# Reordering the first layer of a Fourier / spatial-gating encoder: gate columns, special column and first output block

## The chip, the cores and the metric

The kernel runs on all eight cores of one Trainium2 chip, each core on one sequence of the batch. The metric is the device time of the slowest core, in microseconds. A program on eight cores has executions in a second, slower state (in e1 below, one of 1837.86 us beside three of about 1650); only fast runs are compared here. A ratio below is the mean time of one kernel's fast runs over the mean of the other kernel's fast runs of the same rounds, so it is not quite the ratio of the medians that are quoted beside it. These medians are of the fast runs alone.

## The reference, cut to what matters

```python
def fourier_mixer(h, w_in, w_out):          # layer 0; SEQ 4096, D 1024, E 2048, 8 groups of 256
    proj = h @ w_in
    xin, z = proj[..., :E], proj[..., E:]
    xg = xin.reshape(b, s, 8, 256)
    y = jnp.fft.fft2(xg, axes=(1, 3), norm="ortho").real
    return (y * jax.nn.silu(z)) @ w_out
# layer 1: spatial gating over chunks of 128 positions, w_in (1024, 6144), w_out (2048, 1024)
# before each layer an RMS norm, after each a residual add, at the end an RMS norm
```

The kernel does the Fourier transform with matmuls in two stages: stage 1 over 32 tiles of positions (result U, stored to HBM as Ud), stage 2 after a transposing reload of Ud as V (result H), then for each of eight channel groups a product of H with folded input weights (fold g makes wp from wb; `pq(g)` makes the product). The gate z is 16 columns of channels, each 8 blocks of 8 matmuls (`zall`), with SiLU into one of five buffers `sz`. `gate(g)` multiplies the product into two of these buffers and stores them to HBM as gy. The first output projection (`out0`) reads gy back in blocks of 512 positions as gyt. One real-valued channel per group is a special column, gated apart in `szsp`.

## The kernel before

Only the parts that the change and the argument touch are shown; cuts are marked.

```python
def precast(i):                        # fp32 weights in HBM -> bf16 copies in HBM, software queue
    if i < 2: pool.dma(W0d[:, 8*i:8*i+8, :], w_out0[...], d_pc[i], ...)      # 2 MB written each
    else:     pool.dma(Wind[i-2], w_in1[i-2], d_pc[i], ...)                  # 1 MB written each

for s in range(32):                    # stage 1
    if s + 1 < 32: square(s + 1); norm(s + 1)        # one tile ahead, 3 buffers xn
    # ... 8 transposes, hT, two matmuls with tr, copies to U, store of U ...
    if b8 > 0: zgroup(b8 - 1, s % 2, (s % 8) // 2)   # 8 gate matmuls and a SiLU

def fold(g, dcs):
    # ... matmuls of wb and fmat, copies into wp ...
    if g + 1 < 8: load_wb(2*g + 2); load_wb(2*g + 3) # weights of the next fold, software queue

zall(4)                                # then stage 2: V -> H, eviction in two halves

for g in range(8):
    if g < 7: precast(2*g); precast(2*g + 1)
    # g == 6: special column's gate rows, W0 and x loads
    pq(g); gate(g)
    if g + 1 < 7: fold(g + 1, range(4))
    if g + 2 < 8:
        for zt in (2*g + 4, 2*g + 5):
            if zt > 4: zall(zt)        # gate columns 5.. from group 0 on
    # g == 6: last_column(), gating of szsp on VectorE, its store, load_gy(0, 0, 14)
load_gy(0, 14, 16)                     # then weight ring loads, W1, ...
```

Of the kernel before, what the change touches and what calls it, by code (L numbers as in the profile page):

```python
# [8 lines left out]
BF16 = mybir.dt.bfloat16  # L9
# [178 lines left out]
def build():  # L188
# [30 lines left out]
    with ExitStack() as es:  # L219
# [81 lines left out]
        with ExitStack() as sa:  # L301
# [38 lines left out]
            xn = [tile(f"a0xn{i}", [128, D], BF16) for i in range(3)]  # L340
# [3 lines left out]
            assert top["at"] <= vh + 6 * 8192  # L344
# [5 lines left out]
            wb = [tile("wb0", [128, D], BF16, top["at"] - 2048), tile("wb1", [128, D], BF16)]  # L350
            wp = [tile(f"wp{i}", [128, 8, 256], BF16) for i in range(2)]
# [12 lines left out]
            d_wz = [dsem(f"d_wz{i}") for i in range(4)]  # L364
# [3 lines left out]
            d_sp = dsem("d_sp")  # L368
            zrowb = Buf("zrow")
            Udb = Buf("Ud")  # L370

            def wz_slot(i):
                return i if i < 4 else (i - 4) % 3
# [15 lines left out]
            def square(s):  # L389
                x_, xb = xt[s % NX]  # L390
                j, jb = xn[s % 3]
                ss_, ssb = ss[s % 4]
                act.op(lambda e: e.activation(out=j[:], in_=x_[:], func=AF.Square, scale=1.0 / 32.0,
                                              accum_out=ss_[:]), [xb], [jb, ssb], cost=ca(1024))

            def norm(s):
                x_, xb = xt[s % NX]
                j, jb = xn[s % 3]
# [30 lines left out]
            sp.dma(ident[:], c_id[:, :], d_const, writes=[identb])  # L429
            load_tr(0)  # L430
            load_x(1)
            sp.dma(gT[:], gT_in[:, :], d_cg, writes=[cG])
            load_x(2)
            load_x(3)
            load_tr(1)
            load_x(4)
            sp.dma(cpk[:], c_pk[:, :], d_cA, writes=[cpkb])
            for i in range(4):
                load_wz(i)
            pool.op(lambda e: e.memset(mhalf[:], -0.5), [], [mhalfb])  # L440
            square(0)
            norm(0)
            for s in range(32):
# [3 lines left out]
                if s + 1 < 32:  # L447
                    square(s + 1)
                    norm(s + 1)
                xn_, xnb = xn[s % 3]  # L450
# [17 lines left out]
                sp.dma(Ud[s, 0:128, :], U_[:], d_us[s % 4], reads=[Ub], writes=[Udb])  # L468
                if b8 > 0:
                    zgroup(b8 - 1, s % 2, (s % 8) // 2)  # L470
# [7 lines left out]
            for zt in (3, 0, 1, 2):  # L478
# [5 lines left out]
                else:  # L484
                    load_wz(4 + zt)


            def fold(g, dcs):
                w_, wpb = wp[g % 2]
                for d2 in dcs:  # L490
# [8 lines left out]
                    copy_on(ev_engine(), w_[:, 2 * d2:2 * d2 + 2, :], bank[:].rearrange("p (a b) -> p a b", b=256),  # L499
                            [bb], [wpb])  # L500
                if dcs[-1] == 3:
                    dve.op(lambda e: e.tensor_copy(out=wsp[:, :, g:g + 1], in_=w_[:, :, 128:129]), [wpb], [wspb],
                           waw=False)
                    dve.op(lambda e: e.memset(w_[:, :, 128:129], 0.0), [], [wpb])  # L504
# [4 lines left out]
            def zall(zt):  # L509
# [3 lines left out]
                if zt + 3 < 16:  # L513
                    load_wz(zt + 3)
# [8 lines left out]
            zall(4)  # L523
            for qd in range(7, -1, -1):
                for dc in range(8):
# [8 lines left out]
                    q = ev_engine()  # L534
                    for cs in range(2):
                        scaled(q, H[:, qd, dc, cs, 0:256].rearrange("d (t j k) -> d t j k", j=4, k=2),
                               bank[:].rearrange("d (j c t k) -> d c t j k", c=2, j=4, k=2)[:, cs], sc,
                               [bb, g0sb], [Hb[qd]], 256)
                    if qd == 0:
                        bank, bb = next_f()  # L540
                        pe.op(lambda e: e.matmul(bank[:, 0:64], V[:, 0, dc * 128:(dc + 1) * 128], b64,
                                                 start=True, stop=True), [Vb[0], cpkb], [bb], waw=False)
                        for cs in range(2):
                            scaled(ev_engine(), H[:, :, dc, cs, 256:260],
                                   bank[:, 32 * cs:32 * cs + 32].rearrange("d (q t) -> d q t", t=4), sc, [bb, g0sb],
                                   Hb, 32)
                if qd < 4:
# [3 lines left out]
            def pq(g):  # L551
                w_, wpb = wp[g % 2]
                for qd in range(8):
# [11 lines left out]
                    for o, ob, op in ((Dt, Dtb, ALU.subtract), (St, Stb, ALU.add)):  # L565
                        dve.op(lambda e: e.tensor_tensor(out=o[:, qd, :], in0=pc_[:], in1=bq[:, 0:HQ], op=op),  # L566
                               [pcb, bqb], [ob], waw=False, cost=cd(HQ))

            def gate_tile(o, ob, a_, ab, m_, mb):
# [4 lines left out]
                def mul(out, in0, rb, n):  # L574
                    dve.op(lambda e: e.tensor_tensor(out=out, in0=in0, in1=out, op=ALU.mult), [rb, ob], [ob],
                           waw=False, cost=cd(n))
# [6 lines left out]
            def gate(g):  # L583
                for h, ((a_, ab), (m_, mb)) in enumerate((((Dt, Dtb), (St, Stb)), ((St, Stb), (Dt, Dtb)))):
# [3 lines left out]
                    r0 = (2 * g + h) * 128  # L588
                    sp.dma(gyT[r0:r0 + 128, :], o[:].rearrange("c a b -> c (a b)"), d_gy[i], reads=[ob],
                           writes=[gyTb[2 * g + h]])  # L590

            def last_column():

                for qd in range(8):
# [5 lines left out]
                    copy_on(act, p128[:, qd, :], bank[0:8, 0:HQ], [bb], [p128b], n=HQ)  # L600
# [11 lines left out]
            gytb = [Buf("gyt0", (gyo, gyo + 14336)), Buf("gyt1", (gyo + 14336, gyo + 16384))]  # L612
# [31 lines left out]
            d_g = [dsem(f"d_g{i}") for i in range(2)]  # L644
# [11 lines left out]
            def load_gy(i, k0, k1):  # L656
                bs_ = [gytb[0]] if k1 <= 14 else ([gytb[1]] if k0 >= 14 else gytb)
                sp.dma(gyt[:, k0:k1, :], gyT[k0 * 128:k1 * 128, i * 512:(i + 1) * 512].rearrange(
                    "(kc p) s -> p kc s", p=128), d_g[1 if k0 >= 14 else 0], reads=gyTb[k0:k1], writes=bs_, waw=True)
# [39 lines left out]
            def out0(n, ks, banks):  # L699
                c0 = (n % 4) * 128  # L700
                out_mm(lambda kc: gyt[:, kc, c0:c0 + 128], W0, lambda kc: [gytb[kc // 14]],
                       lambda kc: [W0b[kc // 8]], ks, banks)
# [86 lines left out]

            for g in range(8):  # L790
                if g < 7:
                    precast(2 * g)
                    precast(2 * g + 1)
                if g == 6:
                    sp.dma(szsp[:], zrow.rearrange("g (a b) -> g a b", b=128), d_sp, reads=[zrowb],
                           writes=[szspb], waw=True)
                    for i in range(2):
# [148 lines left out]
```

## Time and profile before

The median of the kernel before was 1708.16 us (1707.06 to 1709.89, three runs). The profiled execution spans 1699.8 us on core 5, the slowest.

The first view shows the busy time of each engine in six stretches of core 5: stage 1 up to the first V load, stage 2 up to the first group product, the groups up to the last gate matmul, the tail up to the first transposition of layer 1, the value tiles of layer 1's first block, and the rest. After the window and its length come busy us and instruction count of each engine, the granted TensorE clock, the DMA share and GB/s.

```profile
core 5: us, PE busy (x) PEld busy (x) DVE busy (x) ACT busy (x) POOL busy (x), PEclk, DMA share, GB/s
0.00:125.30 125.30, 85.18 (x525) 43.01 (x526) 79.17 (x97) 67.63 (x122) 27.90 (x73) 1.00 0.72 221
125.30:195.50 70.20, 51.26 (x397) 28.89 (x396) 27.96 (x75) 35.79 (x90) 4.04 (x8) 0.88 0.66 144
195.50:465.70 270.20, 252.06 (x1570) 154.81 (x1571) 71.10 (x156) 81.86 (x159) 18.06 (x35) 0.96 0.68 131
465.70:564.20 98.50, 69.32 (x465) 45.07 (x464) 33.99 (x62) 15.22 (x35) 4.53 (x9) 0.84 0.80 221
...
595.90:1699.80 1103.90, 1092.52 (x5601) 517.12 (x5599) 536.84 (x782) 305.76 (x505) 89.53 (x178) 1.00 0.36 127
```

The reader sees a kernel bound by TensorE (PE) everywhere but in the first 564 us, where the lengths exceed the PE busy times by 40, 19, 18 and 29 us. Only that is to be won. The waits of PE on the same core say what ended that idle time (total us, number of waits, longest):

```profile
PE pf L681 <- DMA gyt<-gy: 28.3, 2, 15.3
PE pf L415 <- ACT sz_72 L419: 18.1, 1, 18.1
PE pb L454 <- DVE a0xn_57 L405: 17.4, 7, 10.3
PE pb L454 <- DVE a0xn_58 L405: 13.8, 7, 5.7
PE pf L415 <- DMA wz_77<-wz: 12.0, 1, 12.0
...
```

L454 is the transposition of stage 1, which waits for the normalised tile. L415 is a gate matmul: once it waits for its weights (wz), once, for 18.1 us, for a SiLU that itself waits for its buffer. The timeline places that wait after the sixth block of gate column 5, when the six PSUM banks are full (start, length, instruction, count, and in brackets the idle time before it):

```profile
213.14 10.52 PE L415 MATMUL pf<-hT,wz_78 128*128 128x512 bf16 x48
241.79 6.08 PE L415 MATMUL pf<-hT,wz_78 128*128 128x512 bf16 x16 [18.13 <-ACT sz_72 L419]
```

The SiLU waits for the store of the buffer's earlier contents to gy, which was issued at 215.7 us and took 25.3 us to land, beside the two casts of W0. (The casts are the fp32 to bf16 copies of `precast`.) The DMA view has that store; its last number is the time from issue to landing, in us:

```profile
gy<-sz_72 SPq DMA_DIRECT2D x1, 1024.0 KB, 25.3
```

L681 is `out0`, which waits twice for gyt, because the last gate tiles go through HBM and come back.

### The profile page before, as it was taken

How to read it: one execution, taken by the hardware profiler on the slowest of the kernel's cores; microseconds unless marked ns; L12 is line 12 of the kernel's file. 1: busy time of each engine (PE TensorE's matmuls, PEld its weight loads, DVE VectorE, ACT ScalarE, POOL GpSimd, SP SyncE). 2: the span in 40 equal slices, each digit the busy share in tenths (PEclk: the TensorE clock that was granted, in tenths of full speed). 3: DMA queues.
4: the chain of work that ended last, by engine and by line, in shares of the span. 5: the costliest groups of instructions: out<-in, count | busy, mean ns of one | idle time of the engine just before them, and what ended most of it. 6: DMA issues, size and time to landing. Idle time of an engine off the chain costs nothing.

```text
span 1699.8 us, 25579 instructions; the slowest of 8 cores (1683.4 to 1699.8 us)
## 1 busy us (share of the span) xinstructions
PE 1580.3 (93%) x8714; PEld 803.4 (47%) x8714; DVE 768.5 (45%) x1198; ACT 516.9 (30%) x928; POOL 149.1 (9%) x310
## 2 busy tenths in 40 slices
PE   4886859999984999999999999999999999999997
PEld 2443636666672444444444444444444444444443
DVE  5660712222260572464356346345535724643562
ACT  4652613333320332233133123213312322331331
POOL 2220000000000100110110010001001001100100
PEclk9998979999997999999999999999999999999999
DMA  9759485558569553334244325334332533432311
GB/s 259 225 168 228 52 149 125 125 111 168 113 215 199 192 199 136 112 149 161 87 147 149 126 75 190 122 99 171 138 124 87 187 125 99 174 136 87 119 56 50
DMA packets 59854, 239.36 MB, mean 141 GB/s; under 512 B 5688, under 2 KB 22200, under 8 KB 43320
## 3 DMA queue, kind: packets, MB, share of 16 engines
q1 hardware_dynamic: 53968, 208.10, 36.0%
q0 software_dynamic: 5760, 29.63, 11.2%
q8 instruction: 73, 1.20, 0.3%
q14 instruction: 53, 0.43, 0.1%
HBM read 225.26 MB, written 58.85 MB: 167 GB/s over the span
## 4 chain that ended last, share of the span: by engine, by line
PE 83%; DMA 6%; DVE 5%; issue 3%; ACT 1%; POOL 1%; SPq 0%; DVEq 0%; ACTq 0%; POOLq 0%
PE pf L681 25%; PE pf L757 25%; PE pf L415 11%; PE pf L731 10%; PE pf L559 6%; DMA gy<-sz_72 4%; PE pf L767 2%; DMA wz_77<-wz 1%; DMA a0x_54<-xt 1%; DVE H L520 1%; PE pb L716 1%; PE pf L495 1%; PE pb L454 1%; ACT v_2500 L734 0%; ACT v_2499 L734 0%
## 5 line engine op out<-in xcount | busy, mean ns | idle before, releaser
L681 PE MATMUL pf<-W_2474,gyt 128*128 128x512 bf16 x1024 | 228.7, 384 | 28.3 <-DMA gyt<-gy 28.3
L681 PE MATMUL pf<-W_2485,u 128*128 128x512 bf16 x1024 | 222.3, 379 | 0.0
L681 PEld LDWEIGHTS pf<-W_2474,gyt 128*128 128x128 bf16 x1024 | 100.5, 99 | 149.0 <-issue 34.4
L681 PEld LDWEIGHTS pf<-W_2485,u 128*128 128x128 bf16 x1024 | 100.1, 98 | 120.9
L760 ACT ACTIVATE u<-pf 128x512 bf16<-128x512 f32 x128 | 73.8, 599 | 145.1 <-PE pf L757 129.9
L757 PE MATMUL pf<-h1T,ring_2480 128*128 128x512 bf16 x416 | 95.3, 379 | 0.6 <-DVE TT L838 0.6
L757 PE MATMUL pf<-h1T,ring_2481 128*128 128x512 bf16 x416 | 94.8, 379 | 0.0
L757 PE MATMUL pf<-h1T,ring_2483 128*128 128x512 bf16 x416 | 94.8, 379 | 0.0
L757 PE MATMUL pf<-h1T,ring_2484 128*128 128x512 bf16 x416 | 94.8, 379 | 0.0
L415 PE MATMUL pf<-hT,wz_78 128*128 128x512 bf16 x320 | 73.5, 388 | 18.1 <-ACT sz_72 L419 18.1
L757 PE MATMUL pf<-h1T,ring_2482 128*128 128x512 bf16 x384 | 88.3, 379 | 0.0
L415 PE MATMUL pf<-hT,wz_77 128*128 128x512 bf16 x320 | 75.5, 396 | 12.4 <-DMA wz_77<-wz 12.0
L566 DVE TENSOR_TENSOR Dt<-pc_87,pf 128x260 bf16<-128x260 f32 x32 | 13.6, 425 | 153.4 <-PE pf L559 153.4
L415 PE MATMUL pf<-hT,wz_79 128*128 128x512 bf16 x320 | 70.9, 379 | 0.0
L734 ACT ACTIVATE v_2500<-pf 128x512 f32<-128x512 f32 x64 | 38.2, 597 | 74.7 <-DVE sm_2507 L736 33.8
L559 PE MATMUL pf<-H,wp_83 128*128 128x260 bf16 x512 | 59.1, 278 | 1.6 <-DVE wp_83 L504 1.6
L672 POOL TENSOR_SCALAR sm_2506<-sm_2506 128x1 f32<-128x1 f32 x24 | 5.3, 221 | 629.3 <-ACT xn_0_2486 L695 576.4
L757 PEld LDWEIGHTS pf<-h1T,ring_2484 128*128 128x128 bf16 x416 | 39.7, 98 | 43.4
L757 PEld LDWEIGHTS pf<-h1T,ring_2480 128*128 128x128 bf16 x416 | 39.5, 98 | 43.6 <-issue 1.1
L757 PEld LDWEIGHTS pf<-h1T,ring_2483 128*128 128x128 bf16 x416 | 39.6, 98 | 43.2
L757 PEld LDWEIGHTS pf<-h1T,ring_2481 128*128 128x128 bf16 x416 | 39.6, 98 | 43.2
L719 DVE TENSOR_TENSOR h1T<-pb,gTs 128x1024 bf16<-128x1024 bf16 x32 | 38.7, 1208 | 45.6 <-PE pb L716 45.6
(241 smaller groups left out, 2321.7 us busy)
## 6 DMA issues: line engine op xcount, KB each, us to landing
ring_2480<-wind SPq DMA_DIRECT2D x20, 1024.0 KB, 4.9
ring_2481<-wind SPq DMA_DIRECT2D x19, 1024.0 KB, 5.2
ring_2482<-wind SPq DMA_DIRECT2D x19, 1024.0 KB, 5.3
ring_2483<-wind SPq DMA_DIRECT2D x19, 1024.0 KB, 5.2
ring_2484<-wind SPq DMA_DIRECT2D x19, 1024.0 KB, 5.5
gyt<-gy SPq DMA_DIRECT2D x7, 2048.0 KB, 8.5
wind<-w_in1p POOLq DMA_DIRECT2D x12, 1024.0 KB, 14.6
V<-ud SPq DMA_DIRECT2D x32, 256.0 KB, 20.5
```

What stands on the lines that cost most here:

```text
L415: pe.op(lambda e: e.matmul(bank[:], w[:, dc, :], mv[:, :, hf * 64:hf * 64 + 64], start=(dc == 0), stop=(dc == 7)), [wb_, hTb[b8], hTall], ...
L454: pe.op(lambda e: e.transpose(out=bank[:, dc * 128:(dc + 1) * 128], in_=xn_[:, dc * 128:(dc + 1) * 128], identity=ident[:]), [xnb, identb] ...
L495: pe.op(lambda e: e.matmul(bank[:, h * 256:(h + 1) * 256], wb[kc][0][:, dc * 128:(dc + 1) * 128], fmat[:, kc, :], start=(kc == 0), stop=(k ...
L520: return q.op(lambda e: e.tensor_scalar(out=out_ap, in0=in_ap, scalar1=sc, scalar2=None, op0=ALU.mult), reads, writes, waw=False, cost=cd(n))
L559: pe.op(lambda e: e.matmul(bank[:, 0:HQ], w_[:, dc, cs * 128:(cs + 1) * 128], H[:, qd, dc, cs, :], start=(dc == 0), stop=(dc == 7)), [wpb, ...
L681: pe.op(lambda e: e.matmul(bank[:], lhs(kc), rhs[:, kc, nh * 512:(nh + 1) * 512], start=(kc == 0), stop=(kc == 15)), lb(kc) + rb(kc), [bb] ...
L719: dve.op(lambda e: e.tensor_tensor(out=h1T[:, :, t * 128:(t + 1) * 128], in0=bank[:].rearrange("p (a b) -> p a b", b=128), in1=g1T.rearran ...
L731: pe.op(lambda e: e.matmul(bank[:], h1T[:, dc, t * 128:(t + 1) * 128], r_[:, dc, :], start=(dc == 0), stop=(dc == 7)), [h1Tb[t], rb], [bb] ...
L734: act.op(lambda e: e.activation(out=v_[:, j * 512:(j + 1) * 512], in_=bank[:], func=AF.Gelu_apprx_tanh), [bb], [vb_], waw=False)
L757: pe.op(lambda e: e.matmul(bank[:], r_[:, dc, c0:c0 + 128], h1T[:, dc, :], start=(dc == 0), stop=(dc == 7)), h1Tb + [rb], [bb], waw=False, ...
L760: act.op(lambda e: e.activation(out=out_ap, in_=bank[:], func=func), [bb], wb_)
L767: pe.op(lambda e: e.matmul(bank[:, t * 128:(t + 1) * 128], vhat[t][0][:, ct * 128:(ct + 1) * 128], wsT[:, ct // 2, :], start=True, stop=True),
```

## The change

Its intent: normalise two tiles ahead and defer the early loads of stage 1; compute gate column 4 inside stage 2 and evict stage 2 in whole banks; move the gate columns two to a group behind the second product, so that all are done by group 5; do the special column there too, gated on GpSimd; and feed the last four chunks of the first output block from the gate buffers in SBUF. Not shown below: from fold 1 on, the copies of a fold into wp are all on ScalarE, and the small copy into wsp and the clearing of a column of wp that follow it move from VectorE to GpSimd. The core of the diff:

```diff
-            load_tr(0); load_x(1); ... load_tr(1); load_x(4); cpk; four load_wz      (at the start)
+            load_x(1); load_tr(0); load_x(2); ... load_x(4)
+                if s == 2: load_tr(1); four load_wz
+                if s == 24: cpk; load_wz(4)                                           (fifth slot)
-                if s + 1 < 32: square(s + 1); norm(s + 1)
+                if s + 2 < 32: square(s + 2)          ... and norm(s + 2) after the copies to U
...
-            zall(4)
             for qd in range(7, -1, -1):               (stage 2)
-                    two evictions of 256 columns, permuted
+                    one eviction of 512 columns; the permutation moves to the Dt/St writes of pq
+                zgroup((7 - qd) // 2, (7 - qd) % 2, 4)
...
+            zafter = [[], [5, 6], [7, 8], [9, 10], [11, 12], [13, 14, 15], [], []]
+            npre = [0, 2, 4, 6, 9, 12, 14, 14, 14]
             for g in range(8):
-                if g < 7: precast(2 * g); precast(2 * g + 1)
                 pq(g)
                 gate(g)
+                for i in range(npre[g], npre[g + 1]): precast(i)
                 if g + 1 < 7: fold(g + 1, range(4))
-                two gate columns, from g = 0 on
+                for zt in zafter[g]: (fold 7 before column 15) zall(zt)
+                if g == 5: szsp load, last_column(), gating of szsp on pool, W0, load_gy(0, 0, 12), x
...
-            out0: lhs gyt[:, kc, ...]
+            out0: lhs sz[kc % 5] if first block and kc >= 12 else gyt[:, kc, ...]
-            pool.dma(W1 ...), sp.dma(bsB ...)          right after the groups
+            the same two loads after the first output block
```

More of the change, by code (lines that the diff above doesn't have):

```diff
@@ L339, in build @@
             trb = [Buf(f"tr{i}", (top["at"] - 8192 + 2048 * i, top["at"] - 6144 + 2048 * i)) for i in range(4)]
-            xn = [tile(f"a0xn{i}", [128, D], BF16) for i in range(3)]
+            xn = [tile(f"a0xn{i}", [128, D], BF16) for i in range(4)]
             U = [tile(f"U{i}", [128, D], BF16) for i in range(4)]
@@ L343, in build @@
             rs = [tile(f"a0rs{i}", [128, 1], F32) for i in range(4)]
-            assert top["at"] <= vh + 6 * 8192
+            assert top["at"] <= vh + 7 * 8192
             top["at"] = vh + 74752
@@ L350, in build @@
             wb = [tile("wb0", [128, D], BF16, top["at"] - 2048), tile("wb1", [128, D], BF16)]
+            wz.append(tile("wz4", [128, 8, 128], BF16, top["at"] + 4096))
             wp = [tile(f"wp{i}", [128, 8, 256], BF16) for i in range(2)]
@@ L363, in build @@
             d_v = [dsem(f"d_v{i}") for i in range(8)]
-            d_wz = [dsem(f"d_wz{i}") for i in range(4)]
+            d_wz = [dsem(f"d_wz{i}") for i in range(5)]
             d_wb = [dsem(f"d_wb{i}") for i in range(2)]
@@ L368, in build @@
             d_sp = dsem("d_sp")
+            d_row = dsem("d_row")
             zrowb = Buf("zrow")
@@ L372, in wz_slot @@
             def wz_slot(i):
-                return i if i < 4 else (i - 4) % 3
+                return i if i < 5 else (i - 5) % 3
             def load_wz(i):
@@ L390, in square @@
                 x_, xb = xt[s % NX]
-                j, jb = xn[s % 3]
+                j, jb = xn[s % 4]
                 ss_, ssb = ss[s % 4]
@@ L397, in norm @@
                 x_, xb = xt[s % NX]
-                j, jb = xn[s % 3]
+                j, jb = xn[s % 4]
                 ss_, ssb = ss[s % 4]
@@ L429, in build @@
             sp.dma(ident[:], c_id[:, :], d_const, writes=[identb])
+            load_x(1)
             load_tr(0)
-            load_x(1)
+            load_x(2)
             sp.dma(gT[:], gT_in[:, :], d_cg, writes=[cG])
-            load_x(2)
             load_x(3)
-            load_tr(1)
             load_x(4)
-            sp.dma(cpk[:], c_pk[:, :], d_cA, writes=[cpkb])
-            for i in range(4):
-                load_wz(i)
             pool.op(lambda e: e.memset(mhalf[:], -0.5), [], [mhalfb])
@@ L442, in build @@
             norm(0)
+            square(1)
+            norm(1)
             for s in range(32):
@@ L446, in build @@
                     load_x(s + 5)
-                if s + 1 < 32:
-                    square(s + 1)
-                    norm(s + 1)
-                xn_, xnb = xn[s % 3]
+                if s == 2:
+                    load_tr(1)
+                    for i in range(4):
+                        load_wz(i)
+                if s == 24:
+                    sp.dma(cpk[:], c_pk[:, :], d_cA, writes=[cpkb])
+                    load_wz(4)
+                if s + 2 < 32:
+                    square(s + 2)
+                xn_, xnb = xn[s % 4]
                 U_, Ub = U[s % 4]
@@ L468, in build @@
                 sp.dma(Ud[s, 0:128, :], U_[:], d_us[s % 4], reads=[Ub], writes=[Udb])
+                if s + 2 < 32:
+                    norm(s + 2)
                 if b8 > 0:
@@ L484, in build @@
                 else:
-                    load_wz(4 + zt)
+                    load_wz(5 + zt)
             def fold(g, dcs):
@@ L498, in fold @@
                                   [wb[kc][1], cpkb], [bb], waw=False, inc=(h == 1 and kc == 1))
-                    copy_on(ev_engine(), w_[:, 2 * d2:2 * d2 + 2, :], bank[:].rearrange("p (a b) -> p a b", b=256),
+                    copy_on(ev_engine() if g == 0 else act, w_[:, 2 * d2:2 * d2 + 2, :], bank[:].rearrange("p (a b) -> p a b", b=256),
                             [bb], [wpb])
                 if dcs[-1] == 3:
-                    dve.op(lambda e: e.tensor_copy(out=wsp[:, :, g:g + 1], in_=w_[:, :, 128:129]), [wpb], [wspb],
-                           waw=False)
-                    dve.op(lambda e: e.memset(w_[:, :, 128:129], 0.0), [], [wpb])
+                    pool.op(lambda e: e.tensor_copy(out=wsp[:, :, g:g + 1], in_=w_[:, :, 128:129]), [wpb], [wspb],
+                            waw=False)
+                    pool.op(lambda e: e.memset(w_[:, :, 128:129], 0.0), [], [wpb])
                     if g + 1 < 8:
@@ L512, in zall @@
                         zgroup(b8, hf, zt)
-                if zt + 3 < 16:
+                if 5 <= zt < 13:
                     load_wz(zt + 3)
@@ L533, in build @@
                               [Vb[qd], cpkb], [bb], waw=False, inc=(jj == 3))
-                    q = ev_engine()
-                    for cs in range(2):
-                        scaled(q, H[:, qd, dc, cs, 0:256].rearrange("d (t j k) -> d t j k", j=4, k=2),
-                               bank[:].rearrange("d (j c t k) -> d c t j k", c=2, j=4, k=2)[:, cs], sc,
-                               [bb, g0sb], [Hb[qd]], 256)
+                    scaled(ev_engine(), H[:, qd, dc, :, 0:256].rearrange("d c (j k) -> d c j k", j=4),
+                           bank[:].rearrange("d (j c k) -> d c j k", c=2, j=4), sc, [bb, g0sb], [Hb[qd]], 512)
                     if qd == 0:
@@ L542, in build @@
                                                  start=True, stop=True), [Vb[0], cpkb], [bb], waw=False)
+                        q = ev_engine()
                         for cs in range(2):
-                            scaled(ev_engine(), H[:, :, dc, cs, 256:260],
+                            scaled(q, H[:, :, dc, cs, 256:260],
                                    bank[:, 32 * cs:32 * cs + 32].rearrange("d (q t) -> d q t", t=4), sc, [bb, g0sb],
                                    Hb, 32)
+                zgroup((7 - qd) // 2, (7 - qd) % 2, 4)
                 if qd < 4:
@@ L565, in pq, with perm, gate_tile @@
                     for o, ob, op in ((Dt, Dtb, ALU.subtract), (St, Stb, ALU.add)):
-                        dve.op(lambda e: e.tensor_tensor(out=o[:, qd, :], in0=pc_[:], in1=bq[:, 0:HQ], op=op),
-                               [pcb, bqb], [ob], waw=False, cost=cd(HQ))
-            def gate_tile(o, ob, a_, ab, m_, mb):
+                        def perm(t_):
+                            return t_[:, 0:256].rearrange("c (j t k) -> c t j k", j=4, k=2)
+                        dve.op(lambda e: e.tensor_tensor(
+                            out=o[:, qd, 0:256].rearrange("c (t j k) -> c t j k", j=4, k=2), in0=perm(pc_), in1=perm(bq),
+                            op=op), [pcb, bqb], [ob], waw=False, cost=cd(HQ))
+                        dve.op(lambda e: e.tensor_tensor(out=o[:, qd, 256:260], in0=pc_[:, 256:260],
+                                                         in1=bq[:, 256:260], op=op), [pcb, bqb], [ob], waw=False,
+                               cost=0.1)
+            def gate_tile(o, ob, a_, ab, m_, mb, q=dve):
                 def main(t_):
@@ L574, in mul @@
                 def mul(out, in0, rb, n):
-                    dve.op(lambda e: e.tensor_tensor(out=out, in0=in0, in1=out, op=ALU.mult), [rb, ob], [ob],
-                           waw=False, cost=cd(n))
+                    q.op(lambda e: e.tensor_tensor(out=out, in0=in0, in1=out, op=ALU.mult), [rb, ob], [ob],
+                         waw=False, cost=cd(n))
                 mul(o[:, :, 0:64].rearrange("c t (q k) -> c t q k", k=8), main(a_), ab, 2048)
@@ L588, in gate @@
                     r0 = (2 * g + h) * 128
+                    if h == 1 and g >= 6:
+                        sp.dma(o[0:1], szsp[g:g + 1], d_row, reads=[szspb], writes=[ob], waw=True)
                     sp.dma(gyT[r0:r0 + 128, :], o[:].rearrange("c a b -> c (a b)"), d_gy[i], reads=[ob],
@@ L599, in last_column @@
                               [wspb, Hb[qd]], [bb], waw=False, inc=(dc == 7))
-                    copy_on(act, p128[:, qd, :], bank[0:8, 0:HQ], [bb], [p128b], n=HQ)
+                    copy_on(act, p128[:, qd, 0:256].rearrange("c (t j k) -> c t j k", j=4, k=2),
+                            bank[0:8, 0:256].rearrange("c (j t k) -> c t j k", j=4, k=2), [bb], [p128b], n=HQ)
+                    copy_on(act, p128[:, qd, 256:260], bank[0:8, 256:260], [bb], [p128b], n=4)
             def span_tile(name, shape, dtype, off):
@@ L611, in build @@
             gyt, _, _ = at("gyt", [128, 16, 512], BF16, gyo)
-            gytb = [Buf("gyt0", (gyo, gyo + 14336)), Buf("gyt1", (gyo + 14336, gyo + 16384))]
+            gytb = Buf("gyt", (gyo, gyo + 16384))
             NX1 = 5
@@ L643, in build @@
             d_w0 = [dsem(f"d_w0_{i}") for i in range(2)]
-            d_g = [dsem(f"d_g{i}") for i in range(2)]
+            d_g = dsem("d_g")
             d_x1 = [dsem(f"d_x1_{i}") for i in range(NX1)]
@@ L656, in load_gy @@
             def load_gy(i, k0, k1):
-                bs_ = [gytb[0]] if k1 <= 14 else ([gytb[1]] if k0 >= 14 else gytb)
                 sp.dma(gyt[:, k0:k1, :], gyT[k0 * 128:k1 * 128, i * 512:(i + 1) * 512].rearrange(
-                    "(kc p) s -> p kc s", p=128), d_g[1 if k0 >= 14 else 0], reads=gyTb[k0:k1], writes=bs_, waw=True)
+                    "(kc p) s -> p kc s", p=128), d_g, reads=gyTb[k0:k1], writes=[gytb], waw=True)
             NW = 12 * 8
@@ L700, in out0, with here @@
                 c0 = (n % 4) * 128
-                out_mm(lambda kc: gyt[:, kc, c0:c0 + 128], W0, lambda kc: [gytb[kc // 14]],
-                       lambda kc: [W0b[kc // 8]], ks, banks)
+                def here(kc):
+                    return n < 4 and kc >= 12
+                out_mm(lambda kc: sz[kc % 5][0][:].rearrange("c a b -> c (a b)")[:, c0:c0 + 128] if here(kc)
+                       else gyt[:, kc, c0:c0 + 128], W0,
+                       lambda kc: [sz[kc % 5][1]] if here(kc) else [gytb], lambda kc: [W0b[kc // 8]], ks, banks)
             def norm1(n):
@@ L787, in finish_tile @@
                 sp.dma(out[n * 128:(n + 1) * 128, :], x_[:], d_out[n % NX1], reads=[xb], writes=[outb])
+            zafter = [[], [5, 6], [7, 8], [9, 10], [11, 12], [13, 14, 15], [], []]
+            npre = [0, 2, 4, 6, 9, 12, 14, 14, 14]
+            gsp = gyT.rearrange("(g r) s -> g r s", r=256)[:, 128, :]
+            ssp = szsp[:].rearrange("c a b -> c (a b)")
             for g in range(8):
-                if g < 7:
-                    precast(2 * g)
-                    precast(2 * g + 1)
-                if g == 6:
+                pq(g)
+                gate(g)
+                for i in range(npre[g], npre[g + 1]):
+                    precast(i)
+                if g + 1 < 7:
+                    fold(g + 1, range(4))
+                for zt in zafter[g]:
+                    if zt == 15:
+                        fold(7, range(4))
+                    zall(zt)
+                if g == 5:
                     sp.dma(szsp[:], zrow.rearrange("g (a b) -> g a b", b=128), d_sp, reads=[zrowb],
                            writes=[szspb], waw=True)
+                    last_column()
+                    gate_tile(szsp, szspb, p128, p128b, p128, p128b, pool)
                     for i in range(2):
@@ L799, in build @@
                                writes=[W0b[i], hTall])
+                    sp.dma(gsp[0:6], ssp[0:6], d_sp, reads=[szspb], writes=gyTb[1:12:2], waw=True)
+                    load_gy(0, 0, 12)
                     for n in range(4):
                         load_x1(n)
-                pq(g)
-                gate(g)
-                if g + 1 < 7:
-                    fold(g + 1, range(4))
-                if g + 2 < 8:
-                    for zt in (2 * g + 4, 2 * g + 5):
-                        if zt > 4:
-                            zall(zt)
-                if g == 5:
-                    fold(7, range(4))
-                if g == 6:
-                    last_column()
-                    gate_tile(szsp, szspb, p128, p128b, p128, p128b)
-                    gsp = gyT.rearrange("(g r) s -> g r s", r=256)[:, 128, :]
-                    ssp = szsp[:].rearrange("c a b -> c (a b)")
-                    sp.dma(gsp[0:7], ssp[0:7], d_sp, reads=[szspb], writes=gyTb[1:14:2], waw=True)
-                    load_gy(0, 0, 14)
-            sp.dma(gsp[7:8], ssp[7:8], d_sp, reads=[szspb], writes=[gyTb[15]], waw=True)
-            load_gy(0, 14, 16)
             for n in range(NR):
@@ L826, in build @@
             pool.op(lambda e: e.memset(ones[:], 1.0), [], [onesb])
-            pool.dma(W1[:], w_out1[:, :, :], d_w1, writes=[W1b], waw=True)
-            sp.dma(bsB[:], b_s.partition_broadcast(128), d_cB[1], writes=[bsBb], waw=True)
             def tables():
@@ L862, in build @@
                     trans1(2)
+                    sp.dma(bsB[:], b_s.partition_broadcast(128), d_cB[1], writes=[bsBb], waw=True)
+                    pool.dma(W1[:], w_out1[:, :, :], d_w1, writes=[W1b], waw=True)
                 else:
```

## The prediction

> **What bounds the kernel now.** TensorE. The page gives PE 1580 of 1699.8 us; by the windows view PE is busy 1121 of 1133 us from 567 us on (second layer), hardly touched. The other 107 idle us lie in the first 567 us. Waits view and timeline:
> - Transform stage 1, 0 to 123 us: PE 83 us. It waits for normalised tiles (17.4 + 13.8 + 8.3 us), first because x shares the DMA with early weights (landed at 5.6, 14.6, 18.9, 20.8, 25.2 us), then in pairs of 6.73 us, of which PE fills about 5.3: the next square queues on ScalarE behind SiLU.
> - 136.7 to 148.7: 12.0 us on a gate weight load; then 13.8 us of gate matmuls before stage 2, while its V loads run from 125 to 172 us.
> - Stage 2, 165 to 195.5: evictions bound it (DVE 28.0, ACT 27.4, PE 23.2 of 30.1 us).
> - 223.7 to 241.8: 18.1 us. SiLU waits for its buffer's store to gy, which takes 25.3 us beside the W0 cast copies.
> - Tail, 504 to 567: two waits of 13.0 and 15.3 us for gyt, through gate, store and reload.
>
> **What changes, costed.**
> 1. Early loads deferred, normalisation two tiles ahead: first eight tiles about 9 us sooner; later iterations from 3.36 to about 2.85 us (PE needs 2.65, DVE 2.5, ACT 2.45; DMA 768 KB each, estimated 270 GB/s against 306 GB/s seen at 20 to 40 us). Stage 1 ends near 103 instead of 122.7. Gain 19.
> 2. The fifth gate weight has its own slot (12 us wait gone), and that gate column's eight groups of 1.73 us are spread over stage 2, whose 16 half evictions per block (0.37 to 0.40 us) become 8 full ones (about 0.6). Stage 2 then needs 4.7 us of PE per block, about the 5.5 us pace at which V lands. First group product starts near 159, not 195.5. Cumulative gain 36.
> 3. Gate columns move behind the second product, so the 18.1 us wait goes. But the W0 casts (27 and 44.5 us to landing) start with the first product, now without 27 us of gate work to hide them, and the third fold's weights queue behind them on the software queue (30.5 us to landing now). I expect a new wait of about 13 us before fold 2, and 2 us before the second product. Net gain near zero to 5.
> 4. Special column moves before product 6. Its gating moves to GpSimd: the Trainium skill, "GPSIMD Engine Reference", section 3.1, gives 4497 ns for a 2048-element fp32 add; estimate from it about 10 us for 4096 elements, against 5.3 us on DVE here. No run shows this. It should hide under products 6 and 7 (28.4 us), with gyt about 3 us early. Output blocks 0 to 3 read the last four chunks from SBUF, so both gyt waits vanish: gain about 33.
> 5. W1's load moves after the first output block and meets ring loads: loses 0 to 4 us. Permuted Dt/St writes add DVE work off the path.
>
> **Sum.** About 76 us: span near 1624, time **1632 us**, 80% range 1612 to 1656. Faster by over 2%: 0.96; within: 0.03; slower: 0.01.
>
> **What would show it.** V loads begin near 105 us; no gate-weight wait; first product near 159; PE wait before fold 2 on a wb load; no gyt wait over 5 us; second layer's first block near 490.
>
> **What would make it wrong.** Stage 1 being DMA bound (loses 10); a slow GpSimd gate blocking the DMA queue ahead of gyt (5 to 10); W0 casts ending sooner (gains 10); W1 starving the weight ring.

## The result, and the profile after

The changed kernel took 1660.59 us (median of four, 1659.45 to 1663.09) against 1708.49 us for the kernel before (now the median of four runs): ratio 0.9722, 95% interval 0.9705 to 0.9739. It is faster, but 28.6 us slower than predicted and 4.6 us outside the stated range.

The same six stretches on core 7, the slowest of its profiled execution, with the boundaries at the same events:

```profile
core 7: us, PE busy (x) PEld busy (x) DVE busy (x) ACT busy (x) POOL busy (x), PEclk, DMA share, GB/s
0.00:108.40 108.40, 82.02 (x524) 43.78 (x525) 79.28 (x97) 66.41 (x122) 29.88 (x74) 0.94 0.89 258
108.40:166.00 57.60, 48.95 (x399) 29.67 (x397) 22.89 (x38) 33.03 (x62) 3.09 (x7) 0.94 0.79 170
166.00:450.70 284.70, 251.95 (x1585) 155.29 (x1586) 76.48 (x240) 85.50 (x163) 23.35 (x50) 0.95 0.70 125
450.70:518.00 67.30, 64.98 (x449) 43.74 (x448) 30.79 (x88) 13.66 (x39) 12.02 (x12) 0.97 0.74 247
...
549.70:1659.40 1109.70, 1094.61 (x5601) 517.78 (x5599) 537.24 (x782) 306.12 (x506) 89.60 (x178) 0.99 0.36 128
```

| stretch | before, us | after, us | change | predicted change |
|---|---|---|---|---|
| stage 1 | 125.3 | 108.4 | -16.9 | about -20 |
| stage 2 | 70.2 | 57.6 | -12.6 | about -16 |
| groups | 270.2 | 284.7 | +14.5 | 0 to -5 |
| tail | 98.5 | 67.3 | -31.2 | about -33 |
| after it | 1135.6 | 1141.4 | +5.8 | 0 to +4 |

The changes sum to 40.4 us, the difference of the two profiled spans; the timed medians differ by 47.9, since the profiled execution of the kernel before was among its quicker ones. (The last row is the fifth and sixth stretch together. Fold 7, 1.75 us, moved from the tail into the groups, so the groups lost 12.7 us of their own and the tail won 29.5.) The row that is off is the groups. The waits of PE on core 7:

```profile
PE pf L503 <- DMA wb_82<-wbT: 25.8, 1, 25.8
PE pb L460 <- DVE a0xn_57 L407: 17.3, 3, 9.4
PE pf L779 <- DMA ring_2414<-wind: 5.1, 1, 5.1
PE pb L460 <- DVE a0xn_60 L407: 4.9, 2, 4.4
PE pf L503 <- DMA wb_83<-wbT: 3.3, 1, 3.3
...
```

The gyt, SiLU and gate-weight waits are gone. A new one leads: fold 2 (L503) waits 25.8 and 3.3 us for its two weight tiles. The timeline of PE shows it between the second product and column 5 (the 2.20 us before the second product, for the clearing on GpSimd, are the small wait that the prediction named):

```profile
184.27 14.35 PE L565 MATMUL pf<-H,wp_86 128*128 128x260 bf16 x128 [2.20 <-POOL wp_86 L512]
224.46 0.37 PE L503 MATMUL pf<-cpk,wb_82 128*128 128x256 bf16 x1 [25.84 <-DMA wb_82<-wbT]
228.12 0.37 PE L503 MATMUL pf<-cpk,wb_83 128*128 128x256 bf16 x1 [3.29 <-DMA wb_83<-wbT]
...
231.27 14.21 PE L417 MATMUL pf<-hT,wz_78 128*128 128x512 bf16 x64
```

The timeline of GpSimd, which issues the software queue, shows what stands in front of those two loads:

```profile
167.38 1.07 POOL L181 DMA_DIRECT2D w0d<-w_out0p  x2
...
184.46 0.55 POOL L181 DMA_DIRECT2D wb_82<-wbT  x1 [0.45 <-issue]
185.00 0.54 POOL L181 DMA_DIRECT2D wb_83<-wbT  x1
185.53 1.00 POOL L181 DMA_DIRECT2D wind<-w_in1p  x2
```

The DMA view of 184 to 206 us gives the times from issue to landing (the last number, us) of the two weight tiles and of three of the gate stores that run at the same time on the hardware queue:

```profile
...
gy<-sz_73 SPq DMA_DIRECT2D x1, 1024.0 KB, 31.3
gy<-sz_74 SPq DMA_DIRECT2D x1, 1024.0 KB, 35.4
...
gy<-sz_76 SPq DMA_DIRECT2D x1, 1024.0 KB, 39.8
wb_82<-wbT POOLq DMA_DIRECT2D x1, 256.0 KB, 39.7
wb_83<-wbT POOLq DMA_DIRECT2D x1, 256.0 KB, 43.0
```

A 256 KB load that lands in 5.2 us at best in this same kernel took 39.7 us. The cores are not alike in this: 0, 2, 4 and 6 wait 16.6 to 20.1 us before fold 2, and 1, 3, 5 and 7 wait 27.6 to 29.3. In every fast run of this kernel one core of each pair 0/1, 2/3, 4/5, 6/7 ends 7 to 26 us after its neighbour, and not always the same one. The Trainium skill ("Trainium Kernel Development and Optimization", NeuronCore Architecture) gives main storage per pair of cores; the pattern agrees with two cores competing there, but no run here isolates it.

### The profile page after: what moved, and what is told of

It reads as the page before. It is cut to its first block, busy times and chain, and to the rows that moved or that the text cites. A ratio compares the mean times of both kernels' runs of the same rounds, so it can differ in the third digit from the quotient of the medians.

```text
span 1659.4 us, 25674 instructions; the slowest of 8 cores (1633.4 to 1659.4 us)
## 1 busy us (share of the span) xinstructions
PE 1572.5 (95%) x8714; PEld 804.7 (48%) x8714; DVE 766.1 (46%) x1271; ACT 515.4 (31%) x907; POOL 163.7 (10%) x330
## 4 chain that ended last, share of the span: by engine, by line
PE 86%; DMA 7%; DVE 3%; issue 1%; ACT 1%; SPq 1%; POOL 0%; DVEq 0%; ACTq 0%; POOLq 0%
PE pf L697 27%; PE pf L779 25%; PE pf L417 11%; PE pf L753 11%; PE pf L565 6%; DMA wb_83<-wbT 3%; PE pf L789 2%; DMA V<-ud 1%; DMA ring_2414<-wind 1%; DMA a0x_52<-xt 1%; PE pf L503 1%; PE pb L738 1%; SPq L181 1%; DMA a0x_50<-xt 1%; DMA gTs<-gT 1%
## 5 line engine op out<-in xcount | busy, mean ns | idle before, releaser
L697 PE MATMUL pf<-W_2408,gyt 128*128 128x512 bf16 x992 | 218.8, 379 | 0.0
L697 PEld LDWEIGHTS pf<-W_2408,gyt 128*128 128x128 bf16 x992 | 96.6, 98 | 113.4
L575 DVE TENSOR_TENSOR Dt<-pc_89,pf 128x256 bf16<-128x256 f32 x32 | 13.5, 421 | 198.1 <-PE pf L565 198.1
L417 PE MATMUL pf<-hT,wz_78 128*128 128x512 bf16 x320 | 72.2, 384 | 0.0
L417 PE MATMUL pf<-hT,wz_79 128*128 128x512 bf16 x320 | 70.9, 379 | 0.0
L756 ACT ACTIVATE v_2434<-pf 128x512 f32<-128x512 f32 x64 | 38.2, 598 | 75.3 <-DVE sm_2441 L758 34.1
L779 PEld LDWEIGHTS pf<-h1T,ring_2418 128*128 128x128 bf16 x416 | 39.7, 98 | 43.4
L779 PEld LDWEIGHTS pf<-h1T,ring_2415 128*128 128x128 bf16 x416 | 39.7, 98 | 43.2
L793 DVE SCALAR_TENSOR_TENSOR ytmp_2427<-pf,gTs,TT 128x512 f32<-128x512 f32 x64 | 48.1, 751 | 24.8 <-PE pf L789 24.8
L782 ACT ACTIVATE sg_2436<-pf 128x512 bf16<-128x512 f32 x64 | 38.3, 598 | 68.0 <-PE pf L779 54.7
```

Source lines behind the costliest of these rows:

```text
L417: pe.op(lambda e: e.matmul(bank[:], w[:, dc, :], mv[:, :, hf * 64:hf * 64 + 64], start=(dc == 0), stop=(dc == 7)), [wb_, hTb[b8], hTall], ...
L697: pe.op(lambda e: e.matmul(bank[:], lhs(kc), rhs[:, kc, nh * 512:(nh + 1) * 512], start=(kc == 0), stop=(kc == 15)), lb(kc) + rb(kc), [bb] ...
L756: act.op(lambda e: e.activation(out=v_[:, j * 512:(j + 1) * 512], in_=bank[:], func=AF.Gelu_apprx_tanh), [bb], [vb_], waw=False)
L779: pe.op(lambda e: e.matmul(bank[:], r_[:, dc, c0:c0 + 128], h1T[:, dc, :], start=(dc == 0), stop=(dc == 7)), h1Tb + [rb], [bb], waw=False, ...
L782: act.op(lambda e: e.activation(out=out_ap, in_=bank[:], func=func), [bb], wb_)
L793: dve.op(lambda e: e.scalar_tensor_tensor(out=y_[:].rearrange("c (t p) -> c t p", p=128), in0=bank[:].rearrange("c (t p) -> c t p", p=128) ...
```

## The experiments

The theory, called Q: the wait before fold 2 is queueing. The weights stand behind the W0 casts on one software queue, and the casts are slower than I had costed because the gate stores now run beside all of them. The rival, B: the stretch is bound by the bytes of casts and stores together, so that another order only moves the wait. Beside these, one part of the change was undone at a time to see what each was worth. Each diff is against the changed kernel unless it says otherwise. Of fourteen kernels, all were correct but e3, which is wrong on purpose. In the trace lines of the experiments, buffer numbers are left out by the profile.

### e1: casts one group later

```diff
-npre = [0, 2, 4, 6, 9, 12, 14, 14, 14]
+npre = [0, 0, 2, 4, 6, 9, 12, 14, 14]
```

> The changed kernel with the W0 casts issued one group later, so that the weights of fold 2 stand in front of them on the software queue; same bytes, same engines' work. Theory Q (the 29 us wait before fold 2 on the slowest core is queueing behind the casts): that wait falls below 3 us; the gate stores now meet the casts, so SiLU may wait up to 10 us for its buffer; time 1633 to 1645. Rival B (the stretch is bound by the bytes that stores and casts move): the wait only moves to SiLU or to another load, 20 us or more, time 1655 to 1663.

Measured: 1652.00 us (three fast runs, one slow), ratio 0.9695 (0.9666 to 0.9724). The waits of core 7, the slowest:

```profile
PE pf L697 <- DMA gyt<-gy: 10.1, 1, 10.1
PE pf L697 <- DMA sz<-szsp: 5.7, 1, 5.7
...
PE pf L503 <- DMA wb<-wbT: 2.7, 2, 1.8
```

The weight wait fell from 29 to 2.7 us, as Q says, but the time fell by little, as B says. The reason can be read off: the shift had pushed the last two casts into group 6, behind the gating of the special column on GpSimd (issued at 443.0 us), where they delayed the store of the special rows; gyt could be requested only at 464.7 us. The test had a flaw, so its time did not decide. Its trace does show the queueing. On core 7 the weights of fold 2 were issued at 181.7 us, 1 us before the two W0 casts, and landed early (median of the two tiles):

```profile
wb<-wbT POOLq DMA_DIRECT2D x2, 256.0 KB, 8.4
```

That is 8.4 us in front of the same casts, against 39.7 and 43.0 us behind them in the changed kernel.

### e2: one cast in front instead of two

```diff
+npre = [0, 1, 3, 5, 7, 10, 12, 14, 14]
```

> Only one of the two W0 casts stays in front of fold 2's weights. Q: the wait falls by about the time of one cast (17 to 24 us) to 5 to 12 us; time 1640 to 1650. B: the wait stays above 20 us, because the same bytes are on the way in this stretch.

Measured: 1646.96 us, ratio 0.9666 (0.9643 to 0.9689). The weight waits were at most 4.6 us, below what Q expected, and the tail had the same gyt wait as e1 (9.0 us on core 1, the slowest), from the same flaw (its last two casts are in group 6 as well).

### e3: no gate stores in groups 0 and 1 (wrong result on purpose)

```diff
+                    if g >= 2:
                         sp.dma(gyT[r0:r0 + 128, :], o[:]..., d_gy[i], ...)
-                gyt[:, k0:k1] <- gyT rows of chunks k0..k1
+                gyt[:, 0:4] and gyt[:, 4:k1] <- gyT rows of chunks 4..7 and 4..k1
```

> The four gate stores of groups 0 and 1 left out (wrong result on purpose; the loads of the output blocks read other rows instead, same bytes), queue order as in the changed kernel. Q: the wait before fold 2 shrinks only by what the stores slow the casts, from 29 to 15 to 22 us; time 1646 to 1654. B: it falls below 8 us; time below 1642.

Measured: 1645.11 us, ratio 0.9658 (0.9637 to 0.968), just under the time that Q had given. On core 6, the slowest:

```profile
PE pf L503 <- DMA wb<-wbT: 15.5, 2, 13.9
```

With the queue order unchanged and only the four stores gone, the weight wait is 15.5 to 17.1 us on the slower core of each pair and 9.7 to 12.3 on the other. So about 13 us of the 29 came from the stores, and about 15 from the casts alone. On the slower cores this is the range Q had given for the wait, and far from B's 8 us.

What the stores slow can be read from the times to landing of the W0 tensors. The last number is the longest, that of the later W0 cast: first core 7 of the changed kernel, then core 6 of e3.

```profile
DMA to landing us min/median/max: 8.8/18.2/51.8
DMA to landing us min/median/max: 7.5/18.3/43.9
```

Without the stores the later cast took 43.9 us, as in the kernel before (44.5); with them, 51.8. The weights behind it are slowed as well: the two waits of fold 2 ended about 4.8 and 8.4 us after that cast had landed in the changed kernel, and about 2.3 and 4.3 us after it in e3. On cores 0, 2, 4 and 6 of the changed kernel the later cast took only 38.2 to 42.1 us (36.7 to 40.0 on the quicker cores of e3), so there most of what the stores cost lies in the weights.

### e4: W1 loaded later

```diff
-                    pool.dma(W1[:], w_out1[:, :, :], d_w1, ...)       after the first output block
+                    the same line after the value tiles and tables()
```

> W1's load issued after the first value tiles and the tables instead of before them. If the 4 to 7 us wait for the weight ring in the first block comes from W1's load, it goes, and the time falls by 3 to 6 us to about 1655; if it comes from the other loads of that stretch (ring, gyt, bias), the wait and the time stay.

Measured: 1652.43 us, ratio 0.9702 (0.9675 to 0.9729). The ring wait, 4.4 to 6.9 us on six of the eight cores of the changed kernel, is at most 1.9 us. Against the changed kernel's 0.9722 the intervals overlap; e10 below has the clean comparison.

### e6: as e1, with nothing moved into the tail

```diff
+npre = [0, 0, 3, 6, 9, 12, 14, 14, 14]
```

> As e1 (no cast before the weights of fold 2), but the later casts are packed three to a group so that the last two are issued where the changed kernel issues them. Theory Q (queueing behind the casts costs the 29 us; what e1 lost again came from its two last casts being pushed into the tail): no wait over 3 us before fold 2, no gyt wait over 3 us in the tail, time 1632 to 1641. Rival B (the bytes must be paid for somewhere): the tail is clean but a wait of 8 us or more shows in groups 1 to 4, time 1647 or more.

Measured: 1645.10 us (three fast runs of 1645.01, 1645.10 and 1648.86 us, two slow), ratio 0.9647 (0.9596 to 0.9699). The tail was clean, but a wait came back, now before fold 3, since three casts stood in front of its weights. On core 6:

```profile
252.72 0.37 PE L503 MATMUL pf<-cpk,wb 128*128 128x256 bf16 x1 [11.33 <-DMA wb<-wbT]
255.97 3.36 PE L503 MATMUL pf<-cpk,wb 128*128 128x256 bf16 x15 [2.87 <-DMA wb<-wbT]
```

By its wait this is B; the time lies between the two expectations. But it is again a weight load behind casts on the same queue, so the question was whether an order exists with none of these waits.

### e9 and e9_again: two casts in group 1, three in each of groups 2 to 5

```diff
+npre = [0, 0, 2, 5, 8, 11, 14, 14, 14]
```

> No cast before fold 2's weights, two W0 casts in group 1, three of the later casts in each of groups 2 to 5, none in the tail. e6 had put three casts in front of the weights of fold 3 and e1 had put two casts in the tail; this one does neither. Theory Q: no weight wait over 4 us in any group, no gyt wait over 3 us, time 1631 to 1640, ratio to before 0.955 to 0.961. Rival B (the bytes come due somewhere): 1646 or more again.

Measured: 1639.05 us, ratio 0.9626 (0.9607 to 0.9644): the time that Q gave, the ratio just outside. To compare it with the changed kernel on one chip, both ran again together.

> The changed kernel unaltered, as the reference on this chip. Ratio to before 0.970 to 0.974 as recorded; wait before fold 2 of 24 to 30 us on the slower core of each pair and 16 to 21 us on the other.

> e9 unaltered. If the reorder wins back the whole wait, 23 to 29 us below the changed kernel of the same rounds; if part of it is paid again elsewhere, 13 to 19 us below, and then the traces show in which stretch.

Measured: the changed kernel 1657.37 us (four fast runs, one slow), ratio 0.9733 (0.9713 to 0.9753); e9 1639.05 us, ratio 0.9631 (0.9612 to 0.9651). The means of the fast runs are 1657.0 and 1639.7: 17.4 us won by the order of casts alone, with the same bytes. In the groups stretch the profiled core that was slowest went from 283.6 us (core 0) to 265.0 us (core 4). The weight waits of core 0 of the changed kernel, then the waits of core 4 of e9:

```profile
PE pf L503 <- DMA wb<-wbT: 27.5, 2, 24.2
...
PE pf L503 <- DMA wb<-wbT: 9.9, 4, 4.5
PE pf L779 <- DMA ring<-wind: 6.6, 1, 6.6
```

The weight waits went from 27.5 us in two waits to 9.9 in four small ones, which is 17.6 us less. So B falls as stated: the bytes did not have to be paid for with PE time. Q holds for most of the wait, but not for all of it: a part comes back, because later casts still stand in front of later weights.

### e10: e9 and e4 together, and e12: e10 with the early loads of before

```diff
 e10:
+npre = [0, 0, 2, 5, 8, 11, 14, 14, 14]
-                    pool.dma(W1[:], ...)    after the first output block
+                    the same line after tables()
 e12, besides:
+            tr, cpk and four load_wz at the start again, as in e8
```

> e9 and e4 together. If the two losses are independent, the ring wait is under 2 us as well and the time falls by another 4 to 7 us, to 1625 to 1635.

> e10 with the early loads of the kernel before (as in e8). In e8 the V loads began about 3 us earlier than in the changed kernel, so deferring the loads cost time there; if that holds, 2 to 4 us below e10; if it was chance, the same within 2 us.

Measured: e10 1632.45 us (four fast runs, two slow), ratio 0.9583 (0.9566 to 0.9599), with ring waits of at most 2.3 us; e12 1632.82 us, ratio 0.9586 (0.9571 to 0.9601). The two runs were with e9 (0.9626), so loading W1 later is worth 0.4% there, some 7 us, and the two losses add. Moving the early loads changes nothing in time. Both beat both kernels: 4.1 and 4.2% faster than before, where the change was 2.8%.

### e5: the last chunks through HBM again

```diff
-                    return n < 4 and kc >= 12
+                    return False            and load gyt[:, 12:16] after the groups
```

> Part undone: the first output block takes its last four chunks through HBM again (stored, then loaded into gyt) instead of from the gate tiles. If the SBUF path is what removed the two tail waits, a gyt wait of 10 to 20 us comes back and the time rises by 8 to 20 us over the changed kernel, to 1668 to 1680; if moving the special column and W1 was enough, the time rises by less than 4 us.

Measured: 1675.78 us (three fast runs, one slow), ratio 0.982 (0.9766 to 0.9873). On core 6, the slowest:

```profile
PE pf L697 <- DMA gyt<-gy: 22.5, 1, 22.5
```

The wait came back, a little longer than expected; the time is within what was expected. By the ratios, reading the gate buffers in SBUF is worth about 1% (0.982 less 0.972).

### e7: normalisation one tile ahead

```diff
-                if s + 2 < 32: square(s + 2)   ... norm(s + 2) later
+                if s + 1 < 32: square(s + 1); norm(s + 1)
```

> Part undone: square and normalisation one tile ahead as before, early loads still deferred. If the second tile of lead removed the pairwise waits of stage 1, they come back: V loads begin 12 to 16 us later (near 120 us on the slow cores), time 1671 to 1677. If the deferred loads were the larger part, V loads move by less than 6 us.

Measured: two fast runs of 1678.93 and 1676.6 us, two slow ones; ratio 0.9832 (0.9764 to 0.9899). The V loads began at 121.6 to 126.3 us on the eight cores, as in the kernel before (120.8 to 125.7) and not as in the changed kernel (103.8 to 108.6). On core 7 the waits for normalised tiles are back:

```profile
PE pb L459 <- DVE a0xn L407: 40.2, 19, 9.7
```

The whole gain of stage 1 is the second tile of lead.

### e8: the early loads back at the start

```diff
-    if s == 2: load_tr(1); four load_wz          if s == 24: cpk
+    both at the start, in the order of the kernel before
```

> Part undone: the gate weights, twiddles and constants are loaded at the start again, normalisation still two tiles ahead. If the load order of the first 20 us matters by itself, V loads begin 4 to 8 us later and the time rises by 4 to 8 us; if stage 1 is paced by DMA bytes as a whole, the order moves nothing and the time rises by less than 3 us.

Measured: two fast runs of 1654.01 and 1657.13 us, two slow ones. The traces speak more clearly: the V loads began at 101.1 to 104.9 us, some 3 us sooner than in the changed kernel, where neither theory expected them sooner. The first gate block of stage 1, which comes after the first eight tiles, started at 38.4 to 41.7 us in the kernel before, 38.2 to 42.8 in the changed one and 37.4 to 40.3 here. Deferring the loads won nothing: in the changed kernel the chain of waits of core 7 has 16.8 us for one x tile from 19.8 us on, in the stretch where the twiddles and weights, all issued at tile 2, land; that they delay it is likely, but no run isolates it. As e12 shows, the 3 us do not reach the end either.

### e11: gate columns in the order of before

```diff
+zafter = [[5], [6, 7], [8, 9], [10, 11], [12, 13], [14, 15], [], []]
```

> The changed kernel with one gate column in group 0 and two in each later group, the order of the kernel before (casts as in the changed kernel). If the move only exchanged one wait for another, the wait before fold 2 goes below 5 us, the SiLU wait for its buffer's store comes back with 18 to 26 us, and the time stays within 6 us of the changed kernel. If the move was a loss, the SiLU wait is below 14 us and the time falls to 1650 or less; if it was a gain, the time rises to 1668 or more.

Measured: 1653.51 us, ratio 0.9709 (0.9693 to 0.9724), not clearly different from the changed kernel's 0.9722. On core 6:

```profile
PE pf L417 <- ACT sz L421: 21.2, 1, 21.2
```

No weight wait is left, and the SiLU wait is back. Moving the columns exchanged one wait for another.

### e13: the kernel before, with only its casts moved

```diff
 (against the kernel before)
-    if g < 7: precast(2 * g); precast(2 * g + 1)
+    npre = [0, 0, 2, 5, 8, 11, 14, 14, 14];  for i in range(npre[g], npre[g + 1]): precast(i)
```

> The kernel before with its fourteen casts moved one to two groups later (none in group 0, two, then three to a group, none in groups 6 and 7), nothing else. If its 18 us SiLU wait came from the stores meeting the casts, that wait falls below 4 us and the time by 12 to 18 us, to about 1690; if the store is slow for another reason, the wait stays above 12 us and the time within 5 us of before.

Measured: 1693.33 us (six fast runs, two slow), ratio 0.9949 (0.9932 to 0.9966): a small gain, between the two expectations. The timeline of core 1, the slowest, has both the answer and the reason for the half result:

```profile
218.02 3.61 PE L415 MATMUL pf<-hT,wz 128*128 128x512 bf16 x16 [1.06 <-ACT sz L419]
...
270.68 5.53 PE L415 MATMUL pf<-hT,wz 128*128 128x512 bf16 x16 [8.95 <-ACT sz L419]
```

The 18 us wait is 1.06 us where no casts run. In group 1, where the W0 casts now run, column 7 waits 8.95 us. By the DMA view of that core, the two stores of group 1 took 30.3 us to land (median); the quickest store, in group 0, took 7.2. So the SiLU wait of before and the weight wait of after come from the same transfers: the W0 casts, with the gate stores beside them.

## Why the prediction was wrong, point by point

The direction and the mechanism of every step were right but for one half of step 1. One term, the wait of step 3, was wrong in size by 16 us.

- **Step 3 failed**, in its words: "I expect a new wait of about 13 us before fold 2". The place and the cause were right; the time until fold 2's weights land was costed too short, and the wait measured 29.1 us (25.8 and 3.3) on the slowest core. I had taken the casts' time (27 and 44.5 us to landing) from the trace of before, where two gate stores met only the last half of them. In the changed kernel all four stores of groups 0 and 1 met them: the later cast took 51.8 us, and the weights landed later behind it. e3 measured the term: without these stores the wait is 15.5 us on its slowest core. So the step "gain near zero to 5" became a loss of 12.7 us in the groups. That is 12.7 to 17.7 us of the 28.6 missing (35.4 by the profiled spans, on which the table rests); the differences of the other rows of the table, 2 to 6 us each, make up most of the rest. e11 adds that leaving the gate columns in place would have been no better: its SiLU wait is 21.2 us, and its time about that of the changed kernel.
- **Step 1** was nearly right in sum (16.9 us in the trace against 19 to 20) and wrong in its parts. "First eight tiles about 9 us sooner" did not happen; e8 shows that deferring the loads won nothing. The lead of two tiles won everything (e7): the later tiles went to 2.6 us each on core 7 up to 84 us, the PE's own pace, not to 2.85.
- **Step 2** put the first product at 159 us. On the quicker cores of the pairs it was at 158.2 to 161.0, on the slower ones at 163.6 to 166.0. On core 7 the V loads were 3.4 us later than predicted, PE then waited 3.2 us for V, and after the longest of these waits the next 32 matmuls took 3.50 us where the 32 before had taken 2.07.
- **Step 4** was right: no gyt wait, the tail 29.5 us shorter (33 predicted), and e5 shows that the wait returns without the SBUF path. The GpSimd gating took 8.73 us. The estimate of 10 came from the Trainium skill, "GPSIMD Engine Reference", section 3.1, which gives 4497 ns for an add of 2048 fp32 elements; twice that is 9.0. Here one operand is fp32 and the other bf16, and the 2048-element multiplication took 4.07 us, so this case roughly agrees.
- **Step 5** was at the edge: the ring wait was 5.1 us where 0 to 4 were given, and e4 and e10 show that W1's load caused it.

The queue behaviour behind step 3 could have been looked up. The Trainium skill, "DMA: Bandwidth & Descriptors", section on queues, rings and completion order, says that each DMA engine serves its queue rows in turn, packet by packet. The runs agree in that neither queue stops the other and both slow down: from 184 to 206 us the DMA view gives the software queue 92.0% of the DMA engines' time and the hardware queue 8.6%, while both had work waiting, and the later cast took 51.8 us with the stores and 43.9 without. The taking of turns itself is isolated by no run. I had used this for the stores and not turned it round for the casts.

What stays open: why one core of each pair waits about 9 us longer. Nor was it tried whether the weights of fold 2 would come sooner on the hardware queue, where the stores took 24.3 to 39.8 us in the same stretch. Why e9 won 17.4 us and not the whole 27.5 is not open: the four small weight waits, 9.9 us in sum, account for the difference.

## What to carry to other kernels

Work that is moved away from a transfer also stops hiding it: before moving it, list every load that stands on the same queue behind that transfer, and when each is needed. A duration read from a trace holds for the company the transfer had there; if the change makes other transfers run beside it, cost both directions. Bulk background copies belong behind the small loads that are needed next, and spread thinly; here the order of fourteen issues alone was worth 17 us.

## What the Trainium skill lacked or had wrong

- "DMA: Bandwidth & Descriptors" states the turn-taking of queues but gives no measured slowdown: here a 1 MB SBUF-to-HBM store on the hardware queue landed after 7.2 us where no casts ran (e13, group 0) and after 24.3 to 39.8 us beside casting HBM-to-HBM copies on the software queue (the changed kernel).
- The same page gives no number for what a small load loses behind a long copy on the same queue. Here a 256 KB load took 39.7 us behind two 2 MB casts and 5.2 us at best without them.
- No page among those used gives a figure for a casting copy from HBM to HBM: two of 2 MB written landed about 27.5 us (from their median of 36.0) and 44.5 us after issue in the kernel before, and the later one after 51.8 us in the changed one.
- The pages give storage per pair of cores, and the DMA page halves the bandwidth when both stream; neither says that the pair can be uneven where both cores run only DMAs of the kind used here. One core of each pair ended 7 to 26 us after the other.
